# Two-layer hybrid decoder trunk: the expert stage pipelined over pairs of experts, with work of one kind in blocks, and the residual added outside the accumulators

## The chip, the cores and the metric

One launch on one core of a Trainium2 chip. The metric is the device time of that launch in microseconds. The matmul engine is called PE below, its weight loads PEld, the vector engine DVE, the scalar engine ACT, GpSimd POOL and the engine that issues most transfers SP.

## The reference, cut to what matters

The trunk has two layers of width 1024 over 256 tokens. Each is a mixer (three attention branches) and then a mixture of experts; the change concerns the second half, so only that is shown in code.

```
def moe_ffn(h, router_w, router_b, w1, w3, w2):      # 16 experts, D_MODEL 1024, D_FF 512, two experts per token
    ...                                              # router: group of four, then two experts inside it -> combine (256 x 16)
    y = jnp.zeros_like(hf)
    for e in range(N_EXPERTS):
        y = y + combine[:, e:e + 1] * ((jax.nn.silu(hf @ w1[e]) * (hf @ w3[e])) @ w2[e])
    return y

for l in range(2):
    h = layer_norm(ALPHA * h + mixer(h), ln1_g[l], ln1_b[l])
    h = layer_norm(ALPHA * h + moe_ffn(h, ...), ln2_g[l], ln2_b[l])
```

## The kernel before, in words

**Weights.** All weights come from memory in tiles of 128 x 2048 float32 (1 MB). The class `Stream` keeps a list of tiles to load and a set of slots in on-chip memory: whenever the last matmul that reads a tile has been written down, `done` gives its slot back and `pump` puts the next tile of the list into it. The transfer itself waits for that matmul. A layer's experts need 96 such tiles: per pair of experts 4 for w1, 4 for w3 and 4 for w2 (`moe_srcs`, in just that order). SP issues them in the order of the list, except for six tiles per layer (`ST.late`) that POOL issues. In both layers a buffer called `r` serves as one more slot once the mixer has finished with it (`ST.add(hp, ["r"])`).

**The expert stage** (`moe`) goes over 8 pairs `p` of experts, each expert with room for 64 tokens, so that a pair fills the 128 rows of a tile. `gather` (line 1323) picks the tokens of two pairs by a product with a one-hot matrix `SS` and writes them as `xe`. Then, for every pair:

- `up("w1")`, `up("w3")` (L1549): 32 matmuls each in float32, 128x512 of output, w1 giving `h1` and w3 giving `h3`. The two experts of a pair use the two halves of the array, so the trace shows two records for what takes the time of one.
- L1568 (ACT), L1569 and L1570 (DVE): the gated hidden values `g`, with the slot weights `wsl` (`slot_weights`, L1433) multiplied in.
- L1573: two transposes of the one-hot matrix, copied to `CT`. L1578: four transposes of `g`, copied by ACT to `gT` (L1580).
- the `down` matmuls (L1594): 32 in float32 with w2 as the moving operand. Their sum is split by ACT (L1602) and DVE (L1603) into two parts `yh` and `yl` of a rounded float32 form (F32R here), in which PE needs one pass.
- `combine(p, c)` (L1510 in layer 0, L1515 in layer 1): the products with `CT` that put the rows of pair `p` back to their tokens, 8 (layer 0) or 4 wider (layer 1) F32R matmuls for each half `c`, summed over all pairs in four accumulators `ya` in PSUM, which the trace calls z (layer 0) or y (layer 1).

PE's order is that of the code, moved by a scheduler where it sees room. `combine(p - 1, 0)` stands between the up matmuls and the transposes of pair `p`, `combine(p - 1, 1)` behind those. At pairs 0 and 4 nothing is left to combine there (`combine(3)` comes ahead of a branch, `overflow`, that is taken only if an expert has more than 64 tokens).

**The residual**, ALPHA times the normalised output of the mixer, also goes into the accumulators. `residual(k)` for k = 0 to 7 makes four F32R matmuls (L1418), which transpose 128 columns, an ACT pass that applies scale and shift (`xt`), and matmuls in float32 with the identity that add it to `ya`: one in layer 0 (L1423), two in layer 1 (L1426). Two of the eight are done at the end of pairs 1, 3, 5 and 6.

**The end of a layer.** In pair 7 the second half of the last `down` is cut into two column halves, and `finish` takes the finished accumulators. In layer 0 it copies them to `zf`, ACT and DVE by turns (L1531), and makes the first operands of the next mixer (L296, L297), whose first matmuls are L963; DVE's L370 splits that mixer's weights meanwhile. In layer 1 it takes the statistics of the last normalisation (L1524) straight from the accumulators, and L1624 to L1631 normalise from PSUM into `r`, with gamma and beta as two loads of 0.5 MB (`gb`, L1617).

## Time and profile before

| what | value |
|---|---|
| time, median of 3 runs | 1070.39 us (1069.12 to 1071.18) |
| the profiled execution | 1068.88 us, of which the span from first to last instruction is 1067.2 us |
| PE busy | 1032.4 us, 97% of the span |
| DVE, ACT, POOL busy | 524.1, 431.3 and 38.1 us |
| mean granted clock of PE | 0.993 |
| moved by DMA | 293.88 MB, mean 275 GB/s |
| longest group of instructions | L1549, the up matmuls, 236.6 us |

The profile is that of one execution. An engine's busy time is summed over its instructions, and matmuls overlap in part, so what a group of matmuls costs is read from the start of one row to the start of the next. An "x" ahead of a number is the count of records.

### The profile page before, as it was taken

The numbers are of one execution on the slowest core, as the hardware profiler recorded it, in microseconds if no ns is written. First come the engines' busy times: TensorE is split into PE (matmuls) and PEld (weight loads), VectorE is DVE, ScalarE is ACT, GpSimd is POOL, SyncE is SP. The second block draws the span as 40 slices with busy tenths as digits, with TensorE's granted clock in tenths as the row PEclk, the third lists the DMA queues.
The fourth block names the chain that finished last, engine by engine and source line by source line (L and its number), as shares of the span: only waits on it lengthen the run. The fifth ranks groups of instructions, "written<-read, shape, count | busy, mean of one in ns | idle before, by whom it ended". The sixth has DMA issues, their size and how long they took to land. (4 is left out here: it accounts for less than half of the span.)

```text
span 1067.2 us, 16963 instructions
## 1 busy us (share of the span) xinstructions
PE 1032.4 (97%) x6578; PEld 716.0 (67%) x6578; DVE 524.1 (49%) x1481; ACT 431.3 (40%) x1001; POOL 38.1 (4%) x58
## 2 busy tenths in 40 slices
PE   8999999999989999999999999999999999999995
PEld 7888988999854444444497888799998344434332
DVE  7746778776752111211295467877677220212014
ACT  6563776555322121211266547755553121211111
POOL 0200000000000001000001001000000000000001
PEclk8999999999999999999999999999999999999998
DMA  9664334539879999999455534344587999999951
GB/s 360 249 223 149 119 124 173 197 124 376 317 280 341 422 421 419 419 421 411 167 211 202 189 141 159 132 166 158 217 342 296 330 392 421 421 419 419 420 226 39
DMA packets 45402, 293.88 MB, mean 275 GB/s; under 512 B 5120, under 2 KB 7936, under 8 KB 11776
## 3 DMA queue, kind: packets, MB, share of 16 engines
q1 hardware_dynamic: 43008, 277.88, 67.2%
q0 software_dynamic: 1728, 12.58, 2.9%
q10 hardware_dynamic: 576, 2.24, 0.6%
q8 instruction: 54, 0.88, 0.3%
q14 instruction: 36, 0.29, 0.1%
HBM read 291.63 MB, written 1.05 MB: 274 GB/s over the span
## 5 line engine op out<-in xcount | busy, mean ns | idle before, releaser
L1549 PE MATMUL pt<-wt,xe 128*64 128x512 f32 x1024 | 236.6, 596 | 1.6 <-PEq L1447 1.4
L370 DVE TENSOR_TENSOR wlo<-wt,whi 128x1024 fp32r<-128x1024 f32 (+4 forms) x146 | 167.2, 1148 | 80.5 <-ACT whi L369 74.3
L369 ACT CAST whi<-wt 128x1024 fp32r<-128x1024 f32 (+4 forms) x146 | 143.6, 988 | 144.6 <-PE acc L375 105.8
L374 PE MATMUL acc<-hi,whi 128*128 128x256 f32 x576 | 165.3, 288 | 1.7 <-ACT whi L369 0.8
L376 PE MATMUL acc<-hi,wlo 128*128 128x256 f32 x576 | 163.9, 286 | 0.8 <-DVE wlo L370 0.8
L1549 PEld LDWEIGHTS pt<-wt,xe 128*64 128x64 f32 x1024 | 73.7, 137 | 132.3 <-issue 125.6
L375 PE MATMUL acc<-lo,whi 128*128 128x256 f32 x576 | 162.3, 282 | 0.0
L1594 PE MATMUL pt<-wt,gT 128*64 128x512 f32 (+1 forms) x544 | 114.8, 571 | 2.7 <-ACT gT L1580 2.7
L374 PEld LDWEIGHTS acc<-hi,whi 128*128 128x128 f32 x576 | 108.1, 188 | 7.8 <-issue 3.9
L376 PEld LDWEIGHTS acc<-hi,wlo 128*128 128x128 f32 x576 | 108.3, 188 | 4.2 <-DVE wlo L370 2.1
L375 PEld LDWEIGHTS acc<-lo,whi 128*128 128x128 f32 x576 | 108.7, 189 | 0.0
L1594 PEld LDWEIGHTS pt<-wt,gT 128*64 128x64 f32 x544 | 37.1, 137 | 67.9 <-issue 59.0
L1603 DVE TENSOR_TENSOR yl<-pt,yh 128x512 fp32r<-128x512 f32 (+1 forms) x34 | 22.2, 657 | 112.0 <-ACT yh L1602 112.0
L1602 ACT CAST yh<-pt 128x512 fp32r<-128x512 f32 (+1 forms) x34 | 18.9, 560 | 104.6 <-PE pt L1594 104.6
L374 PE MATMUL acc<-ob,whi 128*128 128x256 f32 x192 | 56.8, 296 | 1.1 <-DVE gt L891 0.8
L1570 DVE SCALAR_TENSOR_TENSOR g<-g,wsl,pt 128x512 f32<-128x512 f32 x16 | 12.0, 747 | 93.1 <-PE pt L1549 93.1
L375 PE MATMUL acc<-ob,whi 128*128 128x256 f32 x192 | 54.2, 282 | 0.0
L376 PE MATMUL acc<-ob,wlo 128*128 128x256 f32 x192 | 54.2, 284 | 0.0
L1575 ACT CAST CT<-pt 128x256 fp32r<-128x256 f32 x16 | 6.0, 372 | 107.2 <-PE pt L1573 107.2
L658 DVE COPY ts<-pt 128x384 f32<-128x384 f32 x56 | 30.5, 551 | 30.7 <-PE pt L627 30.6
L1569 DVE SCALAR_TENSOR_TENSOR g<-g,pt 128x512 f32<-128x512 f32 x16 | 11.0, 686 | 67.3 <-ACT g L1568 67.3
L1568 ACT ACTIVATE g<-pt 128x512 f32<-128x512 f32 x16 | 9.6, 597 | 84.1 <-PE pt L1549 84.1
(403 smaller groups left out, 1819.1 us busy)
## 6 DMA issues: line engine op xcount, KB each, us to landing
wt<-in_mw SPq DMA_DIRECT2D x178, 1024.0 KB, 12.2
wt<-in_wfm SPq DMA_DIRECT2D x38, 1024.0 KB, 4.8
wt<-in_wbr SPq DMA_DIRECT2D x12, 1024.0 KB, 4.8
wt<-in_mw POOLq DMA_DIRECT2D x12, 1024.0 KB, 14.5
wt<-in_wcmp SPq DMA_DIRECT2D x8, 1024.0 KB, 6.6
wt<-in_wout SPq DMA_DIRECT2D x8, 1024.0 KB, 8.2
wt<-in_wdv SPq DMA_DIRECT2D x4, 1024.0 KB, 6.2
wt<-in_wmla SPq DMA_DIRECT2D x4, 832.0 KB, 5.5
```

Source lines behind the costliest of these rows:

```text
L369: X["hi"] = A.copy(hi, src).ins
L370: X["lo"] = V.tensor_sub(lo, src, hi.bitcast(F32)).ins
L374: T.matmul(ps, a[0], b[0], start=start, stop=False)
L375: T.matmul(ps, a[0], b[1], start=False, stop=False)
L376: return T.matmul(ps, a[1], b[0], start=False, stop=stop)
L658: X["ts"] = V.tensor_copy(ts, pt).ins
L1549: i = T.matmul(hh[64 * j:64 * j + 64], xe[p][:, 2 * h + k, j * CAP:(j + 1) * CAP], wt[:, c0:c0 + FF], start=(h == 0 and k == 0), stop=(h = ...
L1569: V.scalar_tensor_tensor(g, g, 1.0, h1, op0=ALU.add, op1=ALU.mult)
L1570: V.scalar_tensor_tensor(g, g, wsl[:, p:p + 1], h3, op0=ALU.mult, op1=ALU.mult)
L1594: T.matmul(v[64 * j:64 * j + 64], gT[:, 2 * h + f, 64 * j:64 * j + 64], w2t[:, c0 + ks[0] * P:c0 + ks[1] * P], start=(h == 0 and f == 0), ...
L1602: X0["yh"] = A.copy(yh[:, d], v).ins
L1603: V.tensor_sub(yl[:, d], v, yh[:, d].bitcast(F32))
```

## The change

- **The order of pairs.** The body of a pair is cut into functions (`up`, `hidden`, `turn`, `slots_T`, `down`), and the loop puts `down(p - 1)` right behind the up matmuls of pair `p`, then `turn(p)` (the transposes of `g`), `slots_T(p)` (the transposed one-hot matrix), and both halves of `combine(p - 1)` in one run. Each function goes through `block`, which lets PE start it only after the one before, so that the scheduler doesn't interleave them. At pairs 0 and 4 the next `gather` and the slot weights stand between the up matmuls and the transposes, and `down` waits for the next pair. Pairs 3 and 7 do their own `down` as well.
- **The transposed one-hot matrix** comes from two F32R matmuls with the identity rather than two float32 transposes.
- **Order of weights.** The list `DOWN` puts the w2 tiles of a pair behind the w1 and w3 tiles of the pair in which `down` is now done.
- **The residual, layer 0.** `residual(k)` ends with ACT's pass, which now writes `zf`; all eight stand in pair 7. `finish` adds: `zf = ya + zf`, on DVE.
- **The residual, layer 1.** No residual matmul is left. The buffer `r` of the mixer stays alive: after pair 4, `affine` loads gamma and beta of the first normalisation (1 MB, by SP) and DVE applies them in four 128x1024 operations; `finish` adds `r * ALPHA + ya` on DVE into `r`, takes the statistics from there, and the last normalisation reads `r` rather than PSUM. `r` is then no weight slot in layer 1.
- **Issue.** The six late tiles per layer go by SP like the others.

```diff
+DOWN = [[], [0], [1], [2, 3], [], [4], [5], [6, 7]]
...
         for p in range(8):
             for nm, src in (("w1", mw1), ("w3", mw3)):
                 o += [((l, nm, p, h), src[l, p, h], 2048) for h in range(4)]
-            o += [((l, "w2", 2 * p + c, h), mw2[l, p, c, h], 2048) for c in range(2) for h in range(2)]
+            for q in DOWN[p]:
+                o += down_srcs(q)
...
-    ST.late = {moe_key(l, 47 + NS - i) for l in range(L) for i in range(6)}
...
-        ST.add(hp, ["r"])
-        ST.pump()
+        last = l + 1 == L
+        if not last:
+            ST.add(hp, ["r"])
+            ST.pump()
...
-            d = gp.tile([P, S], F32, name="xt", bufs=1)
-            A.activation(d, ps, AF.Identity, bias=pca[:, l, KD + k:KD + k + 1], scale=pca[:, l, k:k + 1])
-            if not last:
-                T.matmul(ya[k // 2][:, k % 2], ident, d, start=False, stop=False, skip_group_check=True)
-                return
-            for t in range(2):
-                T.matmul(ya[t][k // 4][:, (k % 4) * P:(k % 4 + 1) * P], d[:, t * P:(t + 1) * P], ident, start=False, stop=False,
-                         skip_group_check=True)
+            A.activation(Z["zf"][:, k], ps, AF.Identity, bias=pca[:, l, KD + k:KD + k + 1], scale=pca[:, l, k:k + 1])
+            return i
+
+        def affine():
+            w = load_gb(mh, 1 + 2 * l, "gt1", nc.sync)
+            for j, op in enumerate((ALU.mult, ALU.add)):
+                for t in range(2):
+                    V.tensor_tensor(out=res[:, t], in0=res[:, t], in1=w[:, j * D:j * D + D], op=op)
...
         def finish(c, ks):
             if last:
                 for t in range(2):
-                    V.bn_stats(sts[t][:, c + ks[0] // 2], ya[t][c][:, ks[0] * P:ks[1] * P])
+                    a, b = ks[0] * P, ks[1] * P
+                    d = res[:, t, 512 * c + a:512 * c + b]
+                    V.scalar_tensor_tensor(d, d, ALPHA, ya[t][c][:, a:b], op0=ALU.mult, op1=ALU.add)
+                    V.bn_stats(sts[t][:, c + ks[0] // 2], d)
                 return
...
-                X0["zf", j] = (V.tensor_copy if j % 2 else A.copy)(Z["zf"][:, 2 * j:2 * j + 2], ya[j]).ins
+                d = Z["zf"][:, 2 * j:2 * j + 2]
+                X0["zf", j] = V.tensor_add(d, ya[j], d).ins
...
+        def block(f, *a):
+            with tc.issue_after(PEQ[-1]) if PEQ else nullcontext():
+                i = f(*a)
+            PEQ.append(getattr(i, "ins", i))
...
-                T.transpose(ps[:, t * P:(t + 1) * P], SSf[p // 2][:, t, p % 2 * P:p % 2 * P + P].bitcast(F32), ident)
+                i = T.matmul(ps, SSf[p // 2][:, t, p % 2 * P:p % 2 * P + P], idb[:, P - P * t:3 * P - P * t], start=(t == 0), stop=(t == 1))
...
+        for p in range(8):
+            hs = [pf.tile([P, FF], F32, name="pt") for _ in range(2)]
+            for nm, hh in zip(("w1", "w3"), hs):
+                block(up, p, nm, hh)
...
+            g = hidden(p, *hs)
+            if p in (0, 4):
+                block(gather, p // 2 + 1)
+                block(slot_weights, p // 2 + 1)
+                block(slots_T, p)
+                block(turn, p, g)
+                if p == 4 and last:
+                    affine()
+                continue
+            block(down, p - 1)
+            block(turn, p, g)
+            block(slots_T, p)
+            if p == 2:
+                block(gather, 2)
+                block(slot_weights, 2)
+            if p == 7 and not last:
+                pool, tag = X0["zf"] = ST.take()
+                Z["zf"] = pool.tile([P, KD, S], F32, name="zf", tag=tag)
+                for k in range(KD):
+                    block(residual, k)
+            for c in range(2):
+                block(combine, p - 1, c)
+            if p in (3, 7):
+                block(down, p)
+            if p == 3:
+                for c in range(2):
+                    block(combine, 3, c)
+                overflow()
+                PEQ.clear()
...
-                d, y = r[:, t, a:b], ya[t][a // 512][:, a % 512:a % 512 + b - a]
+                d = r[:, t, a:b]
...
-                    A.activation(d, y, AF.Identity, bias=nbs[t], scale=rs)
+                    A.activation(d, d, AF.Identity, bias=nbs[t], scale=rs)
...
-                        V.scalar_tensor_tensor(d, y, mu, g, op0=ALU.subtract, op1=ALU.mult)
+                        V.scalar_tensor_tensor(d, d, mu, g, op0=ALU.subtract, op1=ALU.mult)
```

The changed file has other line numbers: L1549 is L1557 there, L1594 is L1600, L1578 is L1575, L1573 is L1583, L1323 is L1324.

**PE, layer 0, pair 2.** Before, this is what PE does behind the down matmuls of pair 1 (first row, 32 records in the trace). The names: pt is any PSUM tile, wt a weight tile, z_3880 the first accumulator, xt the scaled residual.

```order
L1594 MATMUL pt<-wt,gT 64x512 x16
...
L1418 MATMUL pt<-idb,yl 128x256
L1549 MATMUL pt<-wt,xe 64x512 x13
L1423 MATMUL z_3880<-xt,idb 128x256
L1549 MATMUL pt<-wt,xe 64x512 x3
L1433 MATMUL pt<-cbs,SS 128x32 x4
L1549 MATMUL pt<-wt,xe 64x512 x9
L1423 MATMUL z_3880<-xt,idb 128x256
L1549 MATMUL pt<-wt,xe 64x512 x7
```

Now the same pair has its up matmuls in one run, and the down matmuls of pair 1 behind them:

```order
L1557 MATMUL pt<-wt,xe 64x512 x32
L1600 MATMUL pt<-wt,gT 64x512 x16
L1575 MATMUL pt<-idb,g 128x128 x4
L1583 MATMUL pt<-idb,SS 128x256 x2
L1324 MATMUL pt<-SS,yh 128x256
```

The two residual matmuls and the slot weights no longer stand inside the run of up matmuls, and the transposes of `g` have a whole `down` ahead of them.

**SP, layer 1, behind the branch of pair 4.** Before, 20 tiles, then gamma, 8 tiles, the last tile in two halves, then beta:

```order
L99 DMA wt<-in_mw 128x2048 x20
L1617 DMA gb<-in_gb 128x1024
L99 DMA wt<-in_mw 128x2048 x8
L95 DMA wt<-in_mw 128x4x256 x2
L1617 DMA gb<-in_gb 128x1024
```

Now, with the 1 MB that `affine` needs as L216:

```order
L100 DMA wt<-in_mw 128x2048 x8
L216 DMA gb<-in_gb 128x2048
L100 DMA wt<-in_mw 128x2048 x8
L1658 DMA gb<-in_gb 128x1024
L100 DMA wt<-in_mw 128x2048 x12
L1658 DMA gb<-in_gb 128x1024
L100 DMA wt<-in_mw 128x2048
L96 DMA wt<-in_mw 128x4x256 x2
```

One transfer of 1 MB is new, and both small ones stand ahead of the last weight tile.

**DVE, end of layer 0.** Before, from the first half of the last `down` on; two of the four copies to `zf` are DVE's, the other two ACT's:

```order
L1603 TENSOR_TENSOR yl<-pt,yh 128x512
L1531 COPY zf<-z_3881 128x512
L297 SCALAR_TENSOR_TENSOR z<-zf,pc,z 128x256 x4
L1603 TENSOR_TENSOR yl<-pt,yh 128x256 x2
L949 TENSOR_TENSOR gl<-wt,gl 128x1024
L1531 COPY zf<-z_3883 128x512
L370 TENSOR_TENSOR wlo<-wt,whi 128x1024
L297 SCALAR_TENSOR_TENSOR z<-zf,pc,z 128x256 x4
L370 TENSOR_TENSOR wlo<-wt,whi 128x1024 x4
```

Now (L1610 is the yl subtraction, L298 the operand of the next mixer, L371 the split of its weights):

```order
L1539 TENSOR_TENSOR zf<-z_3882,zf 128x512
L298 SCALAR_TENSOR_TENSOR z<-zf,pc,z 128x256
L1539 TENSOR_TENSOR zf<-z_3883,zf 128x512
L298 SCALAR_TENSOR_TENSOR z<-zf,pc,z 128x256
L950 TENSOR_TENSOR gl<-wt,gl 128x1024
L371 TENSOR_TENSOR wlo<-wt,whi 128x1024
L298 SCALAR_TENSOR_TENSOR z<-zf,pc,z 128x256 x2
L371 TENSOR_TENSOR wlo<-wt,whi 128x1024 x2
L298 SCALAR_TENSOR_TENSOR z<-zf,pc,z 128x256 x4
```

All four additions are DVE's, and the last operands of the next mixer (L298) stand behind a `gl` and three `wlo` subtractions of 128x1024.

## Rows read from the trace of the kernel before

**Rows 1.** The page: span; GB/s moved in 40 equal slices of the span.

```profile
span 1067.2 us, 16963 instructions
...
GB/s 360 249 223 149 119 124 173 197 124 376 317 280 341 422 421 419 419 421 411 167 211 202 189 141 159 132 166 158 217 342 296 330 392 421 421 419 419 420 226 39
```

**Rows 2.** Waits of PE: waiter, releaser, total us, times, longest.

```profile
PE pt L1594 <- ACT gT L1580: 2.7, 4, 0.7
PE pt L1578 <- DVE g L1570: 1.9, 4, 0.5
```

**Rows 3.** Timeline of PE, pairs 0, 1: start, us, operation, records [idle].

```profile
322.60 0.44 PE L1573 MATMUL pt<-idb,SS 128*128 128x128 f32 x2
...
324.84 7.09 PE L1594 MATMUL pt<-wt,gT 128*64 128x512 f32 x32 [0.68 <-ACT gT L1580]
...
336.05 13.95 PE L1549 MATMUL pt<-wt,xe 128*64 128x512 f32 x64
349.93 0.39 PE L1510 MATMUL z<-CT,yh 128*128 128x256 f32 x1
...
350.99 0.38 PE L1573 MATMUL pt<-idb,SS 128*128 128x128 f32 x2
351.56 0.36 PE L1510 MATMUL z<-CT,yh 128*128 128x256 f32 x1
...
352.69 7.09 PE L1594 MATMUL pt<-wt,gT 128*64 128x512 f32 x32
```

**Rows 4.** The same timeline, residual of pair 1 and pair 2.

```profile
359.70 0.39 PE L1418 MATMUL pt<-idb,yh 128*128 128x256 f32 x1
...
360.84 6.22 PE L1549 MATMUL pt<-wt,xe 128*64 128x512 f32 x26
366.99 0.70 PE L1423 MATMUL z<-xt,idb 128*128 128x256 f32 x2
367.62 1.93 PE L1549 MATMUL pt<-wt,xe 128*64 128x512 f32 x6
369.48 0.62 PE L1433 MATMUL pt<-cbs,SS 128*128 128x32 f32 x4
370.03 4.51 PE L1549 MATMUL pt<-wt,xe 128*64 128x512 f32 x18
...
378.67 0.38 PE L1510 MATMUL z<-CT,yh 128*128 128x256 f32 x1
```

**Rows 5.** The same timeline, pairs 6 and 7 with their residuals, first and last rows.

```profile
472.91 0.38 PE L1418 MATMUL pt<-idb,yh 128*128 128x256 f32 x1
...
490.52 1.94 PE L1549 MATMUL pt<-wt,xe 128*64 128x512 f32 x8
...
494.93 5.37 PE L1594 MATMUL pt<-wt,gT 128*64 128x512 f32 x24
...
519.06 0.39 PE L1510 MATMUL z<-CT,yh 128*128 128x256 f32 x1
```

**Rows 6.** Transfers from 1000 to 1047 us: GB/s in 40 slices of 1.175 us.

```profile
GB/s 432 411 411 415 443 411 418 432 418 418 390 439 411 432 418 418 425 418 425 407 383 359 362 329 185 29 3 0 0 0 0 14 0 0 0 0 0 0 0 0
```

**Rows 7.** SP's last transfer of weights in layer 1: start, us, kind, count.

```profile
1009.70 5.20 SPq L95 DMA_DIRECT2D wt<-in_mw  x2
```

**Rows 8.** Timeline of PE, end of layer 1: the last down matmuls.

```profile
1049.32 1.95 PE L1594 MATMUL pt<-wt,gT 128*64 128x256 f32 x16
...
1051.87 1.95 PE L1594 MATMUL pt<-wt,gT 128*64 128x256 f32 x16
```

**Rows 9.** Timeline of all engines, last 13 us.

```profile
1055.08 1.45 DVE L1524 BATCH_NORM_STATS2 lnst<-y 128x6 f32<-128x256 f32 x3
...
1058.75 0.75 DVE L1630 SCALAR_TENSOR_TENSOR r<-y,lnmv,gb 128x512 f32<-128x512 f32 x1
...
1059.54 1.14 DVE L1631 SCALAR_TENSOR_TENSOR r<-r,rqy,gb 128x512 f32<-128x512 f32 x1
```

**Rows 10.** The page, costliest groups: the split of the weights on DVE.

```profile
L370 DVE TENSOR_TENSOR wlo<-wt,whi 128x1024 fp32r<-128x1024 f32 (+4 forms) x146 | 167.2, 1148 | 80.5 <-ACT whi L369 74.3
```

## Prediction

> **What bounds the kernel now.** I read the page first, then PE's waits, then PE's timeline through the expert stage, and last the transfers. The page has PE busy for 97% of the span, so what counts is what PE does and not what the others do; its waits in the expert stage are few: 2.7 us for `gT` and 1.9 us for `g`, four times each, that is twice per layer, at pairs 0 and 4 [rows 2]. The time is in the work and its order. The timeline shows what order costs when rows are taken start to start: the 64 records of up matmuls in one run take 349.93 - 336.05 = 13.88 us, the 32 of a `down` 359.70 - 352.69 = 7.01 us [rows 3, 4], or 0.215 us a record and about 0.14 us for the start of a run; but 6 records between two other operations take 369.48 - 367.62 = 1.86 us [rows 4], where 6 x 0.215 is 1.29. A run that is cut at an odd place pays again.

> Close behind PE stand the transfers. During either expert stage the page shows six or so slices at 411 to 422 GB/s [rows 1], without a gap: a tile of 1.05 MB then takes 2.5 us. PE uses an up tile in 13.88 / 8 = 1.74 us. So PE eats tiles faster than they come and lives off those loaded ahead. In layer 1 the flow ends at about 1028.8 us (the slice at 185 GB/s) [rows 6], and PE uses the last half tile in the last of the down matmuls, from about 1052.8 us (half way into the run that starts at 1051.87) [rows 8]. The reserve is 24 us at the end of the stage, and a shorter stage spends it.

> **The change part by part.** Each sum is for one layer.

> *Plain pairs.* In pair 1, 349.93 to 352.69 is 2.76 us for two halves of `combine` and six transposes in between [rows 3]. One run of the 16 combine matmuls and the two F32R ones saves a change to float32 and back. Eight such matmuls between float32 work take 1.06 (349.93 to 350.99), 1.13 (351.56 to 352.69) [rows 3] or 1.14 us (359.70 to 360.84) [rows 4]; if nothing of that were the change, merging would give nothing, and if 0.4 us of each pair were, 0.4. I take 0.2 for each of six pairs: 1.2 us (0 to 2.4).

> *Residual.* Pair 2 with the residual of pair 1 takes 378.67 - 359.70 = 18.97 us; without 13.88 for the up matmuls and 0.55 for the slot weights (370.03 - 369.48) 4.54 us are the residual's [rows 4]. In the same way pair 6: 490.52 + 1.86 - 472.91 = 19.47, less 13.88, 0.55 and some 0.2 for two transposes, 4.84; pair 7, with `down(6)`: 519.06 - 494.93 = 24.13, less 13.88, 7.01 and 0.2, 3.04 [rows 5]. The two done behind pair 3 cut no run: 1.14 and twice 0.63 (367.62 - 366.99) [rows 4], 2.40. Together 14.8 us. Layer 1 loses all of it. Layer 0 keeps 32 F32R matmuls in one run: four times 1.14 at most, 3.7 at 0.115 each, which is what eight in 1.06 us leave when 0.14 is the start; I take 4.0. Gain: 10.8 us in layer 0, 14.8 in layer 1.

> *Pairs 0 and 4.* 322.60 to 324.84 is 2.24 us [rows 3] for the six transposes that take 351.56 - 350.99 = 0.57 in pair 1 [rows 3]. The rest, 1.67, is two waits and the changes around them. Now a `gather` covers the wait for `g`, and the next pair's up matmuls cover the wait for `gT`. If that cover is not there, the 0.5 and 0.7 us of [rows 2] come back. Twice 1.67 is 3.3 us. Slot weights that no longer stand inside a run: 0 to 0.6, I take 0.3.

> So PE's work shrinks by 1.2 + 10.8 + 3.3 + 0.3 = 15.6 us in layer 0, and by 19.6 in layer 1.

> *End of layer 0.* The last operands of the next mixer stand behind a `gl` and three `wlo` subtractions rather than a `gl` and one, 2 x 1.15 = 2.3 us more [rows 10], and two more passes of 128x512 fall to DVE, at the 0.75 of L1630 [rows 9] 1.5 us: 3.8 us if all of it is on the path, nothing if the first matmuls of the mixer, which need earlier operands, cover it. I take 1.5, between the two, since those matmuls run while DVE works. ACT's eight passes for `zf` go beside PE's up and combine work; 0.3 us for the first.

> *End of layer 1.* Two additions of 256 columns come into the chain before the last statistics. Three statistics of that width take 1.45 us, 0.48 each [rows 9]: 1.0 us. The first operation of each final pass reads memory instead of PSUM: L1631, which does so, took 1.14 us where L1630 took 0.75 [rows 9]: 0 to 0.4, three times on DVE. Together 1.0 to 2.6, I take 2.1.

> *Transfers, layer 0.* The flow ends near the 19th slice, about 507 us [rows 1]; the last w2 tile is used after 519.06 + 7 us [rows 5]. Of 19 us, 15.6 go. It holds, and the residual's 4 us in pair 7 ask for no tile. The six tiles that go to SP cost nothing there as long as the flow has no gap: SP's transfers are issued well ahead of landing (the last in layer 1 at 1009.70, some 18 us before the flow ends [rows 6, 7]).

> *Transfers, layer 1.* Here the change adds 1 MB for `affine`, 2.5 us of flow, and takes one slot, so one tile more comes within the stage: 2.5 us, and up to 5 if the first free slots also come later. [...] PE waits 1.9 to 6.4 us; I take 5.0, toward the upper end, as the one thing that I can't see is whether slots come free on time.

> [...]

> **Sum.** Layer 0: -15.6 + 1.5 + 0.3 = -13.8. Layer 1: -19.6 + 5.0 + 2.1 = -12.5. From the span of 1067.2 us [rows 1] that makes 1040.9. The profiled execution was 1068.9 us, 1.7 more than its span, so 1042.6; the median before is 1.5 above the profiled one, which gives about 1044 us.

> **The rivals.**
> - *Transfers never bind.* If slots come free earlier than I think (the up tiles of the next pair are now used 7 us sooner), PE has no wait at the end of layer 1: 1044 - 5 = 1039. For it: the flow needs to end only 5 us sooner. Against: it shows no gap that could be closed [rows 6].
> - *Transfers bind harder.* A gap in the flow near the start of either stage, or tiles at 2.6 us, makes 5 to 8 us more: 1050. SP can make such a gap: it waits at the load for `affine` until its buffer is free, with 20 tiles queued behind. The flow then goes on for as long as what is issued ahead lasts, some 18 us [rows 6, 7].
> - *DVE becomes late.* At the end of layer 0 all 3.8 us are on the path, and in the last layer the four operations of `affine`, 4 x 1.15 us [rows 10], delay `g` of pair 6: 1044 + 2.3 + 4 = 1050.
> - *The other side.* One mechanism: gamma and beta for `affine` land late. DVE then stands at `affine`, `g(6)` behind it, `turn(6)` on PE behind that, and every block of PE behind `turn(6)`, as blocks keep their order. Each us of lateness past the slack, which I put at 13 us, is one us of time; it decides from 13 + 26 = 39 us on, so it needs more than one cause. 1075.
> [...]
> - *Blocks buy nothing.* Cut runs could be dear only in how the trace shows them, and the new order could bring new cuts. Against: the prices are start to start, with nothing idle. Then only the residual's matmuls themselves (4 x 1.14 in layer 1, 8 x 0.63 in each) and the waits would go, 4.6 + 10 + 4.6 - 8.9 for ends and transfers: about 1060.

> **How the numbers follow.** Forecast 0.53, from 1040 to 1048 us by its own bounds; never binds 0.15; binds harder 0.13; DVE late 0.08; blocks buy nothing 0.06; late gamma 0.04, and a slower flow 0.01; that makes faster 0.94, the same 0.02 and slower 0.04. The measurement tells some 0.2%, 2 us, from nothing. All but the last two are faster, though small remains of the fifth and of late gamma would fall within 0.2%. The range that leaves out 2 in 10 goes from 1034, below the second case by the bounds of ends and plain pairs, to 1054.

> **What would show it.** In the profile after, up matmuls of pairs 1 to 7 as runs of 64 records at 13.9 us; no wait of PE for `gT`, and less than 0.5 us for `g`; layer 0's stage shorter by 15 to 16 us up to `down(7)`; the flow of layer 1 ending at 1034 to 1036 less what layer 0 saved, and PE waiting for weight tiles in the up matmuls of pair 7 or in the last `down`, 2 to 6 us; the end of layer 1, from the last matmul on, longer by 1 to 2.6 us. I am wrong if PE waits for tiles in layer 0, or for `g` in pair 6, or if the runs are as cut as before.

## The result, and the profile after

The changed kernel takes 1056.68 us (median of 4 runs, 1055.59 to 1058.08) where the kernel before took 1070.24: a ratio of 0.987, with a 95% interval of 0.986 to 0.989. That is 13.6 us, 1.3%, faster; 26 were forecast, and the range began at 1034 and ended at 1054.

The page of the changed kernel, to be read beside [rows 1]:

```profile
span 1056.4 us, 16800 instructions
...
PE 1012.6 (96%) x6498; PEld 711.9 (67%) x6498; DVE 533.9 (51%) x1493; ACT 424.0 (40%) x991; POOL 31.8 (3%) x46
...
PEclk9999999999999998999989999999999999989997
...
GB/s 356 253 231 150 121 121 180 164 157 358 297 272 317 421 421 420 420 421 420 294 176 218 187 125 157 145 135 181 162 381 282 284 327 421 421 419 420 420 420 92
```

PE's busy time fell by 20 us, the span by 10.8. So the work went away, and a part of the gain went into idle time. PE's waits say where (waiter, releaser, total us, times, longest); they answer to [rows 2], whose two lines are both gone:

```profile
PE pt L1557 <- issue: 12.6, 2, 6.4
PE acc L964 <- DVE z L298: 2.3, 2, 1.8
...
PE acc L964 <- ACT gl L949: 1.0, 1, 1.0
```

L1557 are the up matmuls (L1549 before). They waited twice, 12.6 us in all, and for nothing that the profile names: "issue". PE's timeline shows the place:

```profile
343.02 7.04 PE L1600 MATMUL pt<-wt,gT 128*64 128x512 f32 x32
349.99 0.65 PE L1575 MATMUL pt<-idb,g 128*128 128x128 f32 x4
350.40 0.48 PE L1583 MATMUL pt<-idb,SS 128*128 128x256 f32 x2
...
404.18 7.09 PE L1600 MATMUL pt<-wt,gT 128*64 128x512 f32 x32
...
420.06 15.43 PE L1557 MATMUL pt<-wt,xe 128*64 128x512 f32 x64 [6.41 <-issue]
...
440.51 13.95 PE L1557 MATMUL pt<-wt,xe 128*64 128x512 f32 x64
...
514.99 7.10 PE L1600 MATMUL pt<-wt,gT 128*64 128x512 f32 x46
...
526.36 1.86 PE L964 MATMUL acc<-z,gl 128*128 128x258 f32 x10 [0.98 <-ACT gl L949]
530.01 3.38 PE L964 MATMUL acc<-z,gl 128*128 128x258 f32 x14 [1.79 <-DVE z L298]
...
939.39 16.88 PE L1557 MATMUL pt<-wt,xe 128*64 128x512 f32 x64 [6.18 <-issue]
```

The pipeline itself does what it should: `down` right behind the up matmuls, the transposes of `g` behind it with no wait (349.99), up runs of 64 records. But ahead of pair 4, right behind the branch of `overflow`, PE stands for 6.41 us in layer 0 and 6.18 in layer 1, and the up run that follows takes 15.43 and 16.88 us rather than the 13.88 of [rows 3]. The windows of those microseconds show why it is slow (busy time of PE, PEld, DVE, ACT and POOL, then the granted clock, the DMA share and GB/s):

```profile
414.00:416.00 2.00, 0.00 (x0) 0.00 (x0) 0.00 (x0) 0.00 (x0) 0.00 (x0) 1.00 0.97 406
416.00:418.00 2.00, 0.00 (x0) 0.00 (x0) 0.00 (x0) 0.00 (x0) 0.00 (x0) 0.56 1.05 418
418.00:420.00 2.00, 0.00 (x0) 0.00 (x0) 0.00 (x0) 0.00 (x0) 0.00 (x0) 0.50 1.00 410
420.00:422.00 2.00, 1.94 (x6) 0.79 (x8) 0.00 (x0) 0.00 (x0) 0.00 (x0) 0.50 1.01 414
422.00:424.00 2.00, 2.00 (x10) 0.63 (x8) 0.00 (x0) 0.00 (x0) 0.00 (x0) 0.73 1.03 422
```

All engines stand still while the transfers run at 406 to 418 GB/s. With PE idle the granted clock falls from 1.00 (414 to 416 us) to 0.56 and 0.50; it is still 0.50 from 420 to 422 us, in the next matmuls, and 0.73 from 422 to 424. In layer 1 it is 0.50 from 936 to 944 us.

The trace has PE's branch instructions too, two per layer, under PEldq, PE's sequencer. The view of their line gives the count and then the shortest, median and longest in ns. First the changed kernel, then the kernel before, where PE waited 0.75 and 0.65 us at this place:

```profile
L1453 PEldq COMPARE_BRANCH  x4: 81/2962/6053, 413.3 to 933.4; - x4
```

```profile
L1447 PEldq COMPARE_BRANCH  x4: 64/194/397, 419.9 to 943.6; - x4
...
PE pt L1549 <- PEq L1447: 1.4, 2, 0.8
```

So PE stands in the branch itself, for 6.05 us in layer 0 and 5.83 in layer 1, where the kernel before takes 0.40 at most.

The span's 10.8 us by stretches, each from the start of one row to the start of another: the expert stage up to `down(7)` went from 216.57 to 208.52 us in layer 0 and from 216.55 to 205.16 in layer 1; from there through the next mixer to layer 1's first up matmul it grew from 306.17 to 311.41; the end of layer 1 grew from 22.9 to 24.8; and layer 0's stage began 1.4 us later (the granted clock was 0.50 from 298 to 300 us, in the warm-up matmuls ahead of it, where the kernel before had 1.00). The rows from which the two stages are measured, before and then after (layer 0's end, 514.99, stands in the timeline above):

```profile
305.03 1.94 PE L1549 MATMUL pt<-wt,xe 128*64 128x512 f32 x8
521.60 3.65 PE L1594 MATMUL pt<-wt,gT 128*64 128x512 f32 x16
827.77 1.94 PE L1549 MATMUL pt<-wt,xe 128*64 128x512 f32 x8 [0.15 <-DVE xe L1381]
1044.32 3.65 PE L1594 MATMUL pt<-wt,gT 128*64 128x512 f32 x16
```

```profile
306.47 1.94 PE L1557 MATMUL pt<-wt,xe 128*64 128x512 f32 x8
...
826.40 1.94 PE L1557 MATMUL pt<-wt,xe 128*64 128x512 f32 x8 [0.15 <-DVE xe L1384]
1031.56 3.65 PE L1600 MATMUL pt<-wt,gT 128*64 128x512 f32 x16
```

That is -8.05 - 11.39 + 5.24 + 1.96 + 1.44 = -10.80. Without the two waits and the slow runs behind them (6.41 + 1.55 and 6.18 + 3.00, together 17.1 us) the stages would have lost 16.0 and 20.6 us.

What moves during the wait is shown by the small transfers of queue q8, of the kind "instruction": 53 in the whole run, of 16 KB each. In the changed kernel one stands in the window from 416 to 418 us, inside PE's wait (the columns are packets, MB, share of the engines' time), and none on that queue between 388 and 416:

```profile
q8 instruction: 1, 0.02, 3.4%
```

In the kernel before the packet that answers to it stands between 416 and 417 us, four microseconds ahead of its branch, where PE then waited 0.75 us:

```profile
q8 instruction: 1, 0.02, 6.8%
```

From one such packet to the next some 250 PE records go by on average, matmuls and weight loads counted together (13,000 records, 53 packets): I take one packet for one block of PE's code.

### The profile page after: what moved, and what is told of

The parts are those of the page before. It is cut to its first block, busy times and chain, and to the rows that moved or that the text cites. A ratio compares the mean times of both kernels' runs of the same rounds, so it can differ in the third digit from the quotient of the medians.

```text
span 1056.4 us, 16800 instructions
## 1 busy us (share of the span) xinstructions
PE 1012.6 (96%) x6498; PEld 711.9 (67%) x6498; DVE 533.9 (51%) x1493; ACT 424.0 (40%) x991; POOL 31.8 (3%) x46
## 3 DMA queue, kind: packets, MB, share of 16 engines
q10 hardware_dynamic: 576, 2.24, 0.6%
HBM read 292.68 MB, written 1.05 MB: 278 GB/s over the span
## 5 line engine op out<-in xcount | busy, mean ns | idle before, releaser
L1557 PE MATMUL pt<-wt,xe 128*64 128x512 f32 x1024 | 229.0, 604 | 12.7 <-issue 12.6
L371 DVE TENSOR_TENSOR wlo<-wt,whi 128x1024 fp32r<-128x1024 f32 (+4 forms) x146 | 167.5, 1149 | 83.1 <-ACT whi L370 77.0
L1557 PEld LDWEIGHTS pt<-wt,xe 128*64 128x64 f32 x1024 | 73.4, 139 | 153.5 <-issue 149.2
L1600 PE MATMUL pt<-wt,gT 128*64 128x512 f32 (+1 forms) x544 | 113.7, 568 | 0.0
L1600 PEld LDWEIGHTS pt<-wt,gT 128*64 128x64 f32 x544 | 38.8, 137 | 70.3 <-issue 66.1
L1610 DVE TENSOR_TENSOR yl<-pt,yh 128x512 fp32r<-128x512 f32 (+1 forms) x34 | 22.4, 660 | 105.8 <-ACT yh L1609 103.1
L1382 ACT ACTIVATE xe<-pt,pc 128x128 f32<-128x128 f32 x60 | 24.2, 454 | 55.8 <-PE pt L1324 53.9
## 6 DMA issues: line engine op xcount, KB each, us to landing
wt<-in_mw SPq DMA_DIRECT2D x190, 1024.0 KB, 15.6
```

The source lines that it names most:

```text
L371: X["lo"] = V.tensor_sub(lo, src, hi.bitcast(F32)).ins
L1382: A.activation(x[:, k], pj, AF.Identity, bias=bb, scale=g)
L1557: i = T.matmul(hh[64 * j:64 * j + 64], xe[p][:, 2 * h + k, j * CAP:(j + 1) * CAP], wt[:, c0:c0 + FF], start=(h == 0 and k == 0), stop=(h = ...
L1600: i = T.matmul(v[64 * j:64 * j + 64], gT[:, 2 * h + f, 64 * j:64 * j + 64], w2t[:, c0 + ks[0] * P:c0 + ks[1] * P], start=(h == 0 and f == ...
L1610: V.tensor_sub(yl[:, d], v, yh[:, d].bitcast(F32))
```

## The experiments

**Theory F**: the branch skips the overflow path, and the code behind that path is not on the core when PE takes the branch; its fetch goes through the busy transfers. Whether it is there depends on where the branch falls within the blocks of code, so on how many PE instructions stand ahead of it, and on nothing else in the change. **Theory W**: the wait is for data of pair 4, such as a weight tile, which the new order of loads brings late, and the profile fails to name it.

The first run takes the branch away:

```diff
             if p == 3:
                 for c in range(2):
                     block(combine, 3, c)
-                overflow()
-                PEQ.clear()
```

> The changed kernel with the overflow path left out: its two DVE operations, the branch and the code that it skips (tokens beyond 64 per expert would be lost; no expert has so many here). Theory F (PE waits 6.4 and 6.2 us ahead of the up matmuls of pair 4 because the code behind the skipped path is not there yet and its fetch goes through the busy transfers): no wait there, no stretch at a clock of 0.5 behind it, so 17 us less in the span of 1056.4, given back by 0 to 6 us of waits for weight tiles at the end of layer 1 that the delay had covered: 1039 to 1045. Theory W (the wait is for something that the up matmuls of pair 4 need, a weight tile above all, which the profile does not name): the wait stays, 1055 to 1058.

Measured: 1043.26 us (1041.84 to 1044.25), ratio to the kernel before 0.976 (0.974 to 0.977). The wait is gone, and in its place stand, at the very end of layer 1, the waits for weight tiles that the prediction had put there:

```profile
PE pt L1600 <- DMA wt<-in_mw: 2.2, 4, 0.6
...
PE pt L1557 <- DMA wt<-in_mw: 1.6, 3, 0.6
```

In its timeline they are the last three tiles of the up matmuls of pair 7 and the four of `down(6)`, one tile every 2.5 us:

```profile
996.14 1.94 PE L1557 MATMUL pt<-wt,xe 128*64 128x512 f32 x8 [0.46 <-DMA wt<-in_mw]
998.61 1.94 PE L1557 MATMUL pt<-wt,xe 128*64 128x512 f32 x8 [0.54 <-DMA wt<-in_mw]
1001.11 1.94 PE L1557 MATMUL pt<-wt,xe 128*64 128x512 f32 x8 [0.55 <-DMA wt<-in_mw]
1003.68 1.94 PE L1600 MATMUL pt<-wt,gT 128*64 128x512 f32 x8 [0.64 <-DMA wt<-in_mw]
```

Against W it speaks that the tiles of pair 4 are there without a wait, though PE comes for them earlier, and that the changed kernel's time goes by in the branch instruction and not at a matmul; but leaving out the branch leaves out whatever else might wait in it. The next runs keep the whole kernel and only move the branch within the code. The 16 warm-up matmuls of `warm`, whose result nobody reads, are cut into more and narrower ones:

```diff
         for _ in range(n):
-            i = T.matmul(junk, idb[:, P:2 * P], idb, start=True, stop=True)
+            for c in range(0, 3 * P, 128):        # 192 in the second run, 48 in the third
+                i = T.matmul(junk[:, c:c + 128], idb[:, P:2 * P], idb[:, c:c + 128], start=True, stop=True)
```

> The changed kernel with the 16 warm-up matmuls of 384 columns in each layer's routing cut into 48 of 128 columns: the same columns, but 64 more PE instructions ahead of the branch of layer 0 and 128 ahead of that of layer 1. Theory F: a block of code is 256 instructions long, and the branch now comes that much later behind the last block fetch, so the code is there in time: waits under 1 us as before the change, 1040 to 1046. Theory W: nothing changes, waits of 6.4 and 6.2 us, 1055 to 1058.

> The same with 32 of 192 columns: 32 more PE instructions ahead of the branch in layer 0, 64 in layer 1. Theory F: in layer 0 the fetch has some 2 us more of a lead, so the wait shrinks to 2 to 5 us; in layer 1 it is under 1.5 us. Theory W: waits as they are.

> The kernel before, with each layer's 16 warm-up matmuls of 384 columns cut into 128 of 48 columns: 224 more PE instructions ahead of its first branch and 448 ahead of its second, which puts both branches of the kernel before at about the place within a 256-instruction block where the changed kernel has them. The warm-up itself may take 3 to 5 us more per layer. Theory F: PE waits 4 to 7 us ahead of the up matmuls of pair 4 in both layers, where it waited 0.75 and 0.65, with a stretch at a clock of 0.5 behind: span 1080 to 1092. Theory W: waits under 1 us, span 1070 to 1078.

Measured: with 64 more the waits are 0.75 and 0.65 us, with 32 more 0.75 and 0.73; the long waits are gone from both layers of both, so W is out:

```profile
PE pt L1558 <- PEq L1454: 1.4, 2, 0.8
```

```profile
PE pt L1558 <- PEq L1454: 1.5, 2, 0.8
```

And the kernel before, moved to the bad place, has them (this is its line of waits, 6.50 us in layer 0 and 3.08 in layer 1, the second below the 4 to 7 expected):

```profile
PE pt L1550 <- issue: 9.6, 2, 6.5
```

The times of these three, 1063.4 (1057.66 to 1066.57), 1050.14 and 1135.18 us, are no measure of it (the first and the third lie far above what I expected), since I had the price of the narrow warm-up matmuls wrong: 128 of 48 columns took 25.39 us, at a mean clock of 0.52, where 16 of 384 had taken 3.03 at 1.00 (see the last section). The partial wait that I expected in layer 0 of the second did not come either; 32 instructions are enough.

So the next three shift the code with small matmuls in bfloat16, which cost 1.5 us for 24:

```diff
-        for _ in range(n):
+        for _ in range(n - 4):                    # n - 2 in the second
             i = T.matmul(junk, idb[:, P:2 * P], idb, start=True, stop=True)
+        for _ in range(24):                       # 10 in the second, 132 in the third
+            i = T.matmul(junk[:, 0:P], tri, ones, start=True, stop=True)
```

> The whole changed kernel, overflow path and all; of the 16 warm-up matmuls per layer 12 stay, and 24 small ones in bfloat16 (128x128) follow, so that 40 more PE instructions stand ahead of the branch in layer 0 and 80 in layer 1, at about the same time spent. Theory F (late code): waits of 0.7 to 0.8 us at the branches, no stretch at a clock of 0.5 behind them, tile waits of 3 to 4 us at the end of layer 1 as in the run without the branch: 1043 to 1046. If the lead is still short, a wait of 1 to 4 us in layer 0: 1046 to 1049.

> The whole changed kernel with 14 of the 16 warm-up matmuls and 10 small ones in bfloat16 behind them: 16 more instructions ahead of the branch in layer 0 and 32 in layer 1. Theory F: in layer 1 the same 32 as in layer 0 of the run with 32, which had no long wait there, so 0.6 to 0.8 us; in layer 0 between none and all of the 6.4 us, since a fetch that begins 16 instructions earlier has 1 to 2 us more. If waits hung on anything but the place in the code, both layers would do the same.

> The whole changed kernel with 12 of the 16 warm-up matmuls and 132 small ones in bfloat16: 256 more instructions, one whole block of code, ahead of the branch in layer 0 and 512 in layer 1. The warm-up takes some 5 to 8 us more per layer. Theory F: the branch stands at the same place in its block as in the changed kernel, and the waits of 6.4 and 6.2 us are back (5 to 7 each), with a clock of 0.5 behind them. If any change of code cured it: under 1 us, as in the runs with 32, 40 and 64.

The first, with the whole computation, takes 1048.15 us (1045.68 to 1049.39), a ratio of 0.979 (0.977 to 0.981): 8.5 us better than the change, though above the 1043 to 1046 expected, and, with the one that differs from it in `gl` (below), the best complete kernel of the study. That is 5 us more than without the branch. The branches are not it, with 0.75 and 0.73 us; of the span's 6.9 us more, 2.8 lie between `down(7)` of layer 0 and the next stage, 2.0 in the stage of layer 1, 1.0 ahead of layer 0's stage and 0.8 in it. Rows of PE show what the first two are:

```profile
808.97 3.69 PE L1315 MATMUL o<-idb 128*128 128x384 f32 x12
...
818.94 3.53 PE L1559 MATMUL pt<-wt,xe 128*64 128x512 f32 x8 [1.79 <-DVE mxf L1401]
```

PE waits 1.79 us for `mxf`, a small result of the routing on DVE; the 12 warm-up matmuls take 3.69 us where layer 0's take 2.33, and the first eight records of the stage 3.53 where eight take 1.94 elsewhere. The granted clock is 0.50 to 0.70 from 808 to 812 and from 818 to 822 us, and 1.00 there in the run without the branch. What brings the late `mxf` and the lower clock in this run no run tells. Its line of waits for the branch:

```profile
PE pt L1559 <- PEq L1455: 1.5, 2, 0.8
```

A shift of 16 in layer 0 and 32 in layer 1 (1056.42 us, one run) leaves the whole wait in layer 0 (the line of waits) and none in layer 1 (the timeline):

```profile
PE pt L1559 <- issue: 6.4, 1, 6.4
```

```profile
935.45 10.09 PE L1559 MATMUL pt<-wt,xe 128*64 128x512 f32 x46 [0.73 <-PEq L1455]
```

And a shift by a whole block of 256, and by two in layer 1 (1067.43 us, one run), brings both back:

```profile
PE pt L1559 <- issue: 12.7, 2, 6.5
```

This settles it: 0, 256 and 512 instructions wait, so does 16, and 32, 40, 64, 80 and 128 don't. The kernel before fits the same scale when the matmuls and weight loads ahead of each branch are counted in the traces. The changed kernel has 40 fewer ahead of its first branch and 88 fewer ahead of its second; the kernel before as moved has 264 and 536 more than the changed one, 8 and 24 beyond whole blocks. So its 3.08 us are a place of their own:

| more ahead of the branch than in the changed kernel, without whole blocks | longest branch instruction, us |
|---|---|
| 0 (the changed kernel, and 256 and 512 more) | 5.83 to 6.10 |
| 8 (the kernel before, moved, layer 0) | 6.14 |
| 16 | 6.01 |
| 24 (the kernel before, moved, layer 1) | 2.67 |
| 32 (two cases) | 0.38 and 0.40 |
| 40 to 128, with the kernel before as it was | 0.29 to 0.40 |

One more run is on the end of layer 0, where the forecast allowed 1.8 us. DVE is told to make the operands of the first four column blocks ahead of the `gl` subtraction:

```diff
...
+        with tc.issue_after(X0["zlo", 3]) if "yh" in X0 else nullcontext():
-        V.tensor_sub(gl[:, 1], w[:, 0:4], gl[:, 0].bitcast(F32))
+            V.tensor_sub(gl[:, 1], w[:, 0:4], gl[:, 0].bitcast(F32))
...
```

> The same, and at the end of layer 0 DVE makes the operands of the first four column blocks of the next mixer (L298) ahead of the gl subtraction. Theory H (the 5 us that the end of layer 0 costs come from the order of DVE's queue): PE's wait of 1.8 us at L964 for z is gone, 1.5 to 3 us less than the run before. Rival: PE waits as long for gl instead, or the additions themselves are the limit: within 0.5 us of it.

Measured: 1048.04 us against 1048.15 for the kernel without this edit, so nothing. The longest wait for z is down from 1.8 to 0.7 us, and a new one of 1.6, for `hi` of L338 a little later, takes its place. Theory H is not borne out. As I read it, DVE has the same amount to do in those microseconds, in whichever order; that reading is not tested.

Last, the two halves of the change, without the branch and so without its accidents. The first keeps the residual in the accumulators as before:

```diff
...
-            for c in range(2):
-                block(combine, p - 1, c)
+            k = {2: 0, 3: 2, 5: 4, 6: 6}.get(p)
+            for c in range(2):
+                if k is not None:
+                    block(residual, k + c)
+                block(combine, p - 1, c)
+                if k is not None:
+                    block(res_add, k + c)          # the matmuls in float32 into ya
...
```

> The changed kernel without the overflow path, with its new order of pairs, but with the residual kept in the accumulators as before: in pairs 2, 3, 5 and 6 two residual(k) stand between the halves of combine, each with its matmuls in float32 (8 x 0.63 us in layer 0, 8 x 0.65 in layer 1), r is a weight slot in both layers again, nothing is loaded for gamma and beta ahead of time, and both ends are those of before. Theory P (the prediction's terms): order alone gains 1.2 + 3.3 + 0.3 us a layer, and the residual loses its cuts but keeps 8 x (0.5 + 0.63), 9 of 14.8 us: some 10 us a layer less than the kernel before without its branch, 1046 to 1050, with tile waits under 2 us. Rival R (the gain is nearly all the residual's): 1055 to 1062.

The second is the kernel before with the new residual:

```diff
...
-            if p in (1, 3, 5, 6):
-                k = {1: 0, 3: 2, 5: 4, 6: 6}[p]
-                residual(k)
-                residual(k + 1)
+            if p == 4 and last:
+                affine()
+            if p == 6 and not last:
+                ...
+                for k in range(KD):
+                    residual(k)                    # ends with ACT's pass into zf
...
```

> The kernel before without the overflow path and with its old order of pairs and of weights, but with the residual out of the accumulators as in the change (zf written by ACT at the end of pair 6 and added on DVE in layer 0; r, affine and the added passes in layer 1). Theory P: 10.8 us less in layer 0 and 14.8 in layer 1, given back 4 to 6 at the end of layer 0 and 2 in the last normalisation: 1049 to 1053. Rival O (the order brings most): 1058 to 1065.

> The kernel before with the overflow path left out. Its two waits at the branch were 0.75 and 0.65 us, and the branch takes the place of nothing else: 1 to 2.5 us less than before, 1067 to 1069. If the branch cost the kernel before as much as the changed one, it would be 1050 to 1056.

Measured, with the stage from the first up matmul to `down(7)`:

| kernel, all without the branch | us | stage, layer 0 | stage, layer 1 |
|---|---|---|---|
| the kernel before | 1069.52 (1068.15 to 1071.79) | 216.57 | 216.03 |
| residual only | 1052.61 (1051.98 to 1053.29) | 210.30 | 204.00 |
| order only | 1045.72 (1044.80 to 1049.28) | 204.03 | 204.03 |
| both, the change | 1043.26 (1041.84 to 1044.25) | 200.61 | 201.26 |

For the kernel before the branch costs nothing that can be measured (ratio 0.999, 0.998 to 1.000). Order alone brings 24 us, the residual alone 17, and both 26: they overlap. I read this so that a part of what the residual cost was that it cut the runs, and the new order stops the cutting too: with order alone the up matmuls stand in runs of 64 records again. Order alone came out just below the 1046 to 1050 of theory P; the residual alone within its range, but with 6.3 and 12.0 us of stage rather than 10.8 and 14.8, and less lost at the ends. In that run PE also waits 1.2 us for ACT's pass into `zf`. Both rivals, R and O, are out. In layer 1 the residual, once the order is new, brings 2.8 us of stage, since 3.8 us of tile waits come with it.

## Why the prediction was wrong

**The step that failed** is a term that isn't in the sum: the wait at the branch ahead of pair 4. The prediction names PE's waits in the expert stage and calls them few, without this one; it was 0.75 and 0.65 us before, and the sum leaves it as it was, that is, it puts the change of it at nothing without a reason. The change has 40 and 88 fewer PE instructions ahead of the two branches, and so, as I read the runs, moves them to a place in their block of code where the fetch comes too late (its packet starts 2.6 to 2.8 us ahead of PE's first matmul, and 4.9 to 15.7 us ahead in the short waits): 17.1 us, of which the prediction has nothing. It gives back the 3.8 us of tile waits that it covers, which makes 13.3, and the forecast missed by 12.7. The code without the branch takes 1043.3 us; 1044 was forecast. That this fits so closely is in part luck: with the whole code and the branch only moved it is 1048.15, so 8.5 us of the miss are shown in that way, and for the other 4 that run's profile has the late `mxf` and the stretches at the lower clock.

**PE's work**: 15.6 us less forecast for layer 0, 16.0 found without the wait; 19.6 for layer 1, 20.6 found, and 18.6 between the two kernels without the branch (216.03 - 201.26, and 3.8 of tile waits). The sum was right, and two of its terms can be read in the changed kernel:

```profile
463.99 13.96 PE L1557 MATMUL pt<-wt,xe 128*64 128x512 f32 x64
...
487.47 13.95 PE L1557 MATMUL pt<-wt,xe 128*64 128x512 f32 x64
...
508.95 0.28 PE L1423 MATMUL pt<-idb,yh 128*128 128x256 f32 x1
...
513.00 0.28 PE L1515 MATMUL z<-CT,yh 128*128 128x256 f32 x1
```

A plain pair (pair 6, 463.99 to 487.47) takes 23.48 us, where pair 1 took 359.70 - 336.05 = 23.65 before [rows 3, 4], so 0.17 for 0.2 forecast; the residual's F32R matmuls take 4.05 us for 4.0. In the trace of the kernel before an F32R matmul has one record (L1418, 64 for 64) and one in float32 two (L1423, 16 for 8). But the terms are not what each edit brings alone. In layer 0 order alone brings 12.5 us, where its terms (plain pairs, pairs 0 and 4, slot weights) make 4.8, and the residual alone 6.3 for 10.8. In layer 1 the residual alone brings 12.0, and behind the new order 2.8 and the 3.8 of tile waits, 6.6: so some 5.4 of the 12.0, by this estimate, were the price of where it stood.

**Transfers**: right, and in the place that was named. The tiles are late in the up matmuls of pair 7 and in `down(6)`, 3.8 us where 5.0 was taken from 1.9 to 6.4. The upper end of that, and so the 5.0, counts on up to 2 us between the end of the flow and PE's use of the last tile, which no run shows: in the changed kernel the last half tile landed 0.5 us behind the last packet of the flow (1035.3 and 1034.8 us). In the changed kernel the 9 us lost at the branch of layer 1 let the flow catch up, so that this wait does not show; the run with the long wait in layer 0 alone has it, 2.2 and 1.5 us, and the changed kernel and the run moved by 256, with both long waits, have none. In layer 0 no tile is late. The flow is no slower after the change: 419 to 421 GB/s in the slices that it fills, 419 to 422 before.

**End of layer 1**: 2.1 us forecast, 1.96 found. **End of layer 0**: 1.8 forecast; PE waits 2.8 us at L964, and the stretch to the next stage is 5.2 us longer, 2.9 in the run without the branch. The rest goes with stretches at the lower clock (0.50 from 530 to 534 us, behind the second of these waits), which in these runs come and go with kernels that are the same there; I can't say what puts them where they are.

**The rivals**: none of them was this. The one that warned of a wait in a place that PE comes to in order, late gamma and beta, did not occur: no wait for `g` shows in pair 6.

## What to carry to other kernels

In this kernel the price of a branch hung on how many instructions stood ahead of it: 8.0 and 9.2 us with the clock's part in the changed kernel, a wait of 0.65 to 0.75 us with 32 to 128 more. So an edit that adds or removes some can switch such a price on or off. When a change brings less than its removed work says, look for "issue" waits behind branches, and for the duration of the branch instruction, before doubting the sums, and move the branch by a few dozen cheap instructions to see. And when two edits remove the same stalls, their gains can't be added: try each alone.

## What was not expected of the hardware

- PE's wait at the branch, which I read as one for code, takes 6.2 to 6.5 us in six of the seven long cases in these runs (3.08 in the seventh) while the transfers move more than 400 GB/s, against 0.65 to 0.75 us in the short ones. The branch instruction shows it: 5.83 to 6.14 us (2.67 in the seventh) against 0.29 to 0.40. 16 instructions decide: a shift of 16 still waits in full, one of 32 does not.
- PE idle for 6.41 and 6.18 us came out at a granted clock of 0.50 (418 to 422 and 936 to 944 us); the up run behind it took 1.55 and 3.00 us more.
- What a narrow warm-up matmul in the rounded float32 form cost went with the granted clock in these runs. In the run with 32 more, 32 of 192 columns took 3.80 us in layer 1, at a clock of 1.00, and 6.95 in layer 0, at 0.50 (window columns as above): 0.12 and 0.22 us each, where 16 of 384 took 3.03 at 1.00 in the kernel before, 0.19 each. 48 of 128 columns took 9.45 us and 128 of 48 took 25.39, 0.20 each, the latter at a mean of 0.52 from 298 to 323 us though PE had no gap between them; which is cause and which is effect no run tells.

```profile
813.40 3.80 PE L1316 MATMUL o<-idb 128*128 128x192 f32 x32
813.80:817.40 3.60, 3.60 (x34) 3.60 (x33) 3.40 (x23) 2.15 (x4) 0.00 (x0) 1.00 0.79 253
297.61 6.95 PE L1316 MATMUL o<-idb 128*128 128x192 f32 x32
298.00:304.00 6.00, 6.00 (x30) 6.00 (x30) 3.68 (x25) 2.15 (x4) 0.00 (x0) 0.50 0.85 326
```

```profile
298.00:323.00 25.00, 25.00 (x124) 25.00 (x124) 3.02 (x20) 2.15 (x4) 0.00 (x0) 0.52 0.22 85
```
